# A decoder layer on one core: the prompt's threshold branch inside the sample's index stage, a projection between the first key tile's turn and its products, the gate's transposes one block later

## The chip, the cores and the metric

One core of a Trainium2 chip runs the whole kernel. The metric is device time in microseconds (us) for one execution; lower is better. The engines are named as in the profile: PE (TensorE), DVE (VectorE), ACT (ScalarE), POOL (GpSimd), SP (SyncE, which issues most transfers). PEld are PE's weight loads.

## The reference

One layer of a hybrid decoder for a prompt of 1024 tokens and for a sample step of 8 sequences with 4 new tokens each over a past of 8192 tokens. Model width 1024. The steps that matter here, cut from the reference:

```python
z = einsum('btd,de->bte', rmsnorm(x), w_in)       # qa ka va | qi ki wi | ga | qb kb vb gb
# group A: sparse attention
s = einsum('bqhd,bsd->bqhs', qi, ki) * 64**-0.5
score = einsum('bqh,bqhs->bqs', wi, relu(s)); score = where(valid, score, -inf)
idx = top_k(score, 256)                            # per query; the sample's keys come from paged cache_kidx
oa = softmax attention of qa over the gathered ka, va (with a bias by distance)
# group B: retention, 8 heads, chunks of 128, rotary angles on qb and kb
ob, state = chunked recurrence
y = concat(silu(ga) * oa, silu(gb) * head_norm(ob)) @ w_out
x = x + rmsnorm(y)
out = x + (p @ w_ple_up) * sigmoid(x @ w_ple_gate)
```

The outputs are y of prompt and sample, their k, v and index keys, and the retention states.

## The kernel before, in words

The layer is one program in five stages, here with their times in the profiled execution.

1. Norm, transposes, the index projections and the prompt's scores (0 to 172 us).
2. **The sample's index stage** (172 to 340). For each sequence `b` (8) and half `a` (2) an indirect gather on POOL brings 128 x 2048 past index keys into `kx` (two buffers). For each half tile `up` PE turns it (eight transposes into `ptx`, a pair of PSUM banks), ACT copies it to `kT`, PE multiplies it with the queries (two matmuls into `pox`) and ACT applies relu (`rl`). After four of these, `head_sum` weights and sums the heads (`py`), and `by_key` transposes the sums (`pxt`) and DVE copies them out (`xe`). `pox`, `pxt`, `pfl` and a few others share PSUM's tag "t", which has two banks, so a third user waits until the first has been read. Two other pieces of work are called in this loop at a set rate. `unit(rate)` advances a generator of projections (`proj_b`, PSUM tile `pb`, 24 matmuls each: qa, kava, ga). `step(bp)` advances `bisect_prompt`, which finds for each prompt query the threshold of its 256 best scores, on six query blocks at once, on DVE and for two of the six counts on ACT (`js`).
3. **Retention** (340 to 660): four pairs of heads, `hp` 0 to 3. Each has the projections of q and k (`pqk`, eight blocks, with the rotation `rp` on DVE and `qk` on POOL) and then of v and gate (`pvg`, eight blocks, each with its chunk: `ret`, `second`, `sm`, `sbd`). In `steps(hp)` run what is left of `bisect_prompt` (first pair) and the sample's own selection (`su`, `sjk`, `stot`, a branch at L965, comparisons L1194 and L1195, two running sums `cx` at L1203).
4. Attention (660 to 830), with gathers of the chosen keys on POOL.
5. Output projection (`po`) and gate (`pg`, `pu`), 830 to 1064. After the last column block of the output projection `finish_y(tb)` adds the residual and transposes the result with `split_T` for the gate's matmuls (`pty`).

`bisect_prompt` is a generator of 31 steps. Its last seven are: the flag `many` (PE reduces it into `pfl`, DVE reads it as `flp` and loads it into a register), then `tc.If(many > 0)` with 16 further counts, which the data does not call for, and `tb_`; and after it six mask blocks, one for each query block of 384 to 1024 keys. A block is a count and comparison (L727, L730), a running sum (L731, `rk`), three elementwise steps (L732, L733, L734) and small ones.

```python
            tickb[0] += 1.5          # L817: 16 passes, 24 steps of bisect_prompt in the index stage
            ...
        if hp == 0:
            step(bp, 2)              # L1420: the rest in retention's first pair
```

The order on each engine is not the order of the code. A scheduler places the instructions by its own estimate of times, within the dependences and the buffers; on the chip each engine then runs its queue strictly in that order and waits on semaphores. `tc.issue_after(ins)` adds an order without a wait: what is traced in its block comes behind `ins` on that engine.

Of the kernel before, what the change touches and what calls it, by code (L numbers as in the profile page):

```python
# [120 lines left out]
def tile_step(ctx: ExitStack, tc: tile.TileContext, I, O):  # L121
    nc = tc.nc
# [21 lines left out]
    def bank(name, tag="b"):  # L144
        if tag in kept.get("tags", ()):
            return kept["pool"].tile([128, 512], F32, tag="s", bufs=1, name=name)
        return psum["pool"].tile([128, 512], F32, tag=tag, bufs=psum["bufs"][tag], name=name)

    def pair(name):
        return psum["pool"].tile([128, 1024], F32, tag="S", bufs=psum["bufs"]["S"], name=name)  # L150
# [3 lines left out]
    def C(name, rows=128):  # L154
        o, w = _CW[name]
        return cst[:rows, o:o + w]

    ident = C("ident")
# [217 lines left out]
    tickb = [0.0]  # L376
# [83 lines left out]
    def unit(rate):  # L460
        tick[0] += rate
        while tick[0] >= 1:
            tick[0] -= 1
            next(unit_gen, None)
# [276 lines left out]
    def step(gen, n=1):  # L741
        for _ in range(n):
            next(gen, None)
# [45 lines left out]
    def later():  # L789
        if pend:  # L790
            pend.pop(0)()

    for b in range(8):
        rls = []
        for a in range(2):
            kx = sx.tile([128, 2048], F32, tag="kx", bufs=2, name="kx")
            nc.gpsimd.indirect_dma_start(
                out=kx, out_offset=None, in_=pages,
                in_offset=bass.IndirectOffsetOnAxis(ap=kidx[:, a * 8 + b:a * 8 + b + 1], axis=0))
            for up in range(2):  # L800
                pt = pair("ptx")
                kT = sx.tile([128, 1024], F32, tag="kT", bufs=2, name="kT")
                for u2 in range(2):
                    for i in range(4):
                        r2 = up * 8 + i * 2 + u2
                        c0 = u2 * 512 + i * 128
                        nc.tensor.transpose(pt[:, c0:c0 + 128], kx[:, r2 * 128:(r2 + 1) * 128], ident)
                nc.scalar.copy(kT, pt)
                po = bank("pox", "t")
                for u2 in range(2):  # L810
                    nc.tensor.matmul(po[u2 * 64:u2 * 64 + 64, :], qbd[:, b, :], kT[:, u2 * 512:u2 * 512 + 512],
                                     start=True, stop=True)
                rl = sx.tile([128, 512], F32, tag="rl", bufs=6, name="rl")
                nc.scalar.activation(rl, po, AF.Relu)
                rls.append(rl)
            later()
            tickb[0] += 1.5  # L817
            while tickb[0] >= 1:
                tickb[0] -= 1
                step(bp)  # L820
            unit(1.4)
        pend.append(lambda b=b, rls=rls: head_sum(b, rls))
    while pend:
        later()
# [597 lines left out]
    for hp in range(4):  # L1422
# [13 lines left out]
        for tb in range(8):  # L1436
            pt = bank("pqk")
# [9 lines left out]
        for tb in range(8):  # L1447
            pt = bank("pvg")
# [204 lines left out]
    pt = bank("ptys", "t")  # L1653
# [6 lines left out]
    x2 = [mr.tile([128, D], F32, tag="x2", bufs=9, name=f"x2_{tb}") for tb in range(9)]  # L1660
# [13 lines left out]
    def finish_y(tb):  # L1674
        rows = 128 if tb < 8 else NS
        src = (I["x_prompt"][0, tb * 128:(tb + 1) * 128, :] if tb < 8
               else I["x_sample"].rearrange("b t d -> (b t) d"))
        xt = mr.tile([128, D], F32, tag="xr", bufs=2, name="xr")
        nc.sync.dma_start(xt[:rows], src)
        y = x2[tb]  # L1680
        ss = mg.tile([128, 1], F32, tag="ss", bufs=2, name="ss2")
        nc.vector.tensor_reduce(ss[:rows], ssq[:rows, tb], axis=AX.X, op=ALU.add)
        r = rstd_of(ss, rows, 1.0 / D, f"y{tb}", mg)
        nc.vector.scalar_tensor_tensor(y[:rows], y[:rows], r[:rows], xt[:rows], op0=ALU.mult, op1=ALU.add)
        if tb < 8:
            x2T[tb] = split_T((y[:, :512], y[:, 512:]), 10 + tb)
        else:
            for a in range(2):
                pt = bank("ptxs", "t")
                for j in range(4):  # L1690
                    nc.tensor.transpose(pt[:, j * NS:(j + 1) * NS],
                                        y[:NS, a * 512 + j * 128:a * 512 + (j + 1) * 128], ident[:NS, :NS])
                nc.scalar.copy(x2sT[:, a * 4:a * 4 + 4], pt[:, :4 * NS].rearrange("p (j r) -> p j r", j=4))
# [23 lines left out]
    for cb in range(4):  # L1717
        cs = slice(cb * 256, (cb + 1) * 256)
        for tb in (8, *range(8)) if cb else (0, 1, 2, 3, 8, 4, 5, 6, 7):
            pt = bank("po2")  # L1720
            if tb < 8:
                mm_a(pt, tlhs(yT), wt[cb], 256, tb)
                take_y(tb, cb, pt[:, :256])
            else:
                sh = mm_s(pt, ysT, wt[cb], 256, mg, f"o{cb}")
                take_y(8, cb, sh[:, :256])
                wt.append(load_w(f"o{cb + 1}", [(w_out[:, (cb + 1) * 256:(cb + 2) * 256], 256)]) if cb < 3 else
                          load_w("g0", [(w_gate[:, 0:256], 256)]))
            if cb == 2:
                load_p(tb)  # L1730
            if cb == 3:
                finish_y(tb)

# [12 lines left out]
    for cb in range(4):  # L1748
        cur, curu = wg, wu
        cs = slice(cb * 256, (cb + 1) * 256)  # L1750
        for tb in (8, *range(8)):
            rows = 128 if tb < 8 else NS
            pg, pu = bank("pg"), bank("pu")
            sg = mg.tile([128, 256], F32, tag="sgm", bufs=2, name="sgm")
            if tb < 8:
                mm_a(pg, tlhs(x2T), cur, 256, tb)
                mm_a(pu, plhs, curu, 256, tb, kc=2)
                gsrc, usrc = pg[:, :256], pu[:, :256]
            else:
                gsrc = mm_s(pg, x2sT, cur, 256, mg, f"g{cb}")  # L1760
                nc.scalar.activation(sg[:rows], gsrc, AF.Sigmoid)
                usrc = mm_s(pu, psT, curu, 256, mg, f"u{cb}", kc=2)
                if cb < 3:
                    wg = load_w(f"g{cb + 1}", [(w_gate[:, (cb + 1) * 256:(cb + 2) * 256], 256)])
                    wu = load_up(cb + 1)
            if tb < 8:
                nc.scalar.activation(sg[:rows], gsrc, AF.Sigmoid)
            nc.vector.tensor_tensor(sg[:rows], usrc, sg[:rows], op=ALU.mult)  # L1768
            nc.vector.tensor_tensor(sg[:rows], sg[:rows], x2[tb][:rows, cs], op=ALU.add)
            dst = (O["y_prompt"][0, tb * 128:(tb + 1) * 128, cs] if tb < 8  # L1770
                   else O["y_sample"].rearrange("b t d -> (b t) d")[:, cs])
            nc.sync.dma_start(dst, sg[:rows])
# [38 lines left out]
```

## Time and profile before

| | us |
|---|---|
| median of three runs | 1076.75 |
| lowest, highest | 1073.38, 1078.46 |
| the profiled execution, time | 1065.73 |
| its span | 1063.9 |
| PE busy, share of the span | 991.7, 93% |
| DVE busy | 699.8, 66% |
| ACT busy | 504.2, 47% |
| POOL busy | 288.1, 27% |

The mean granted clock of PE is 0.973. A row of a group or an instruction gives the line, the engine, the operation, `out<-in` by the program's names (buffer numbers left out), the shapes, and in brackets the idle time of that engine just before it with what ended it. A row of waits gives the waiting instruction, what it waited for, the total in us, how often, and the longest. A row of stages gives the length of the stage, the busy us of PE, PEld, DVE, ACT and POOL with the number of instructions, then the granted clock of PE as a share of full speed.

### The profile page before, as it was taken

To read this page: it belongs to the slowest core of one execution; us is meant where nothing else is said; L and a number is where in the kernel's file an instruction comes from. 1 tells how busy PE (TensorE), PEld (TensorE's weight loads), DVE (VectorE), ACT (ScalarE), POOL (GpSimd) and SP (SyncE) were. 2 spreads that over 40 slices of the span, in tenths; PEclk is the share of its full clock that TensorE was granted. 3 is DMA by queue.
4 is the path that set the end of the run, shared out by engine and by line. 5 is a ranking of instruction groups with operands and counts; after the bars stand their busy time and mean duration, and the time that the engine had idled before them with its cause. 6 is when DMAs were issued, how large, how long until landed. Compare 5 with 4: busy or idle time off the path is not lost.

```text
span 1063.9 us, 19686 instructions
## 1 busy us (share of the span) xinstructions
PE 991.7 (93%) x7375; PEld 838.6 (79%) x7375; DVE 699.8 (66%) x2012; ACT 504.2 (47%) x1092; POOL 288.1 (27%) x287
## 2 busy tenths in 40 slices
PE   3899998998999789999989995999999999999998
PEld 2899997676776778898788893666656899989998
DVE  6847768999401798978986957887764424874332
ACT  5445554986434356842333435656544523442211
POOL 3102223111201532423632512634340521222100
PEclk8999999999999989999989996899999999999999
DMA  8211235546343311112201425623211312432211
GB/s 291 65 60 51 79 96 169 186 145 202 126 164 111 70 40 41 37 48 87 61 24 41 119 86 149 190 79 105 75 56 47 117 41 80 148 111 82 86 37 40
DMA packets 98308, 102.24 MB, mean 96 GB/s; under 512 B 21346, under 2 KB 88386, under 8 KB 95906
## 3 DMA queue, kind: packets, MB, share of 16 engines
q1 hardware_dynamic: 92450, 74.74, 23.3%
q0 software_dynamic: 5760, 26.22, 7.9%
q8 instruction: 58, 0.95, 0.4%
q14 instruction: 40, 0.33, 0.1%
HBM read 79.25 MB, written 21.68 MB: 95 GB/s over the span
## 4 chain that ended last, share of the span: by engine, by line
PE 53%; DVE 8%; ACT 2%; DMA 2%; issue 1%; POOL 1%; SPq 0%; DVEq 0%; ACTq 0%; POOLq 0%
PE ob L1587 4%; PE ptp L1579 4%; PE pg L265 3%; PE pg L267 3%; PE pg L266 3%; PE po L265 3%; PE po L266 2%; PE po L267 2%; PE pvg L265 2%; PE pvg L266 2%; PE pvg L267 2%; PE sa L1563 2%; PE sa L1564 2%; PE pqk L265 2%; PE pqk L266 1%; PE pqk L267 1%
## 5 line engine op out<-in xcount | busy, mean ns | idle before, releaser
L1147 POOL DMA_INDIRECT kvs<-in_cache_kv,idx x64 | 63.6, 994 | 84.1 <-ACT pT L1584 44.7
L265 PE MATMUL pqk<-whi_qkb,xh 128*128 128x256 f32 x256 | 74.5, 291 | 5.5 <-DVE rp L1036 5.5
L265 PE MATMUL pvg<-whi_vgb,xh 128*128 128x256 f32 x256 | 77.4, 302 | 1.6 <-DVE need L729 1.5
L266 PE MATMUL pvg<-wlo_vgb,xh 128*128 128x256 f32 x256 | 76.6, 299 | 0.0
L267 PE MATMUL pvg<-whi_vgb,xl 128*128 128x256 f32 x256 | 75.2, 294 | 0.0
L266 PE MATMUL pqk<-wlo_qkb,xh 128*128 128x256 f32 x256 | 73.5, 287 | 0.0
L265 PE MATMUL po<-whi_o,yTh 128*128 128x256 f32 x256 | 73.1, 286 | 0.4 <-DVE yaT L1598 0.4
L267 PE MATMUL pqk<-whi_qkb,xl 128*128 128x256 f32 x256 | 73.0, 285 | 0.0
L267 PE MATMUL po<-whi_o,yTl 128*128 128x256 f32 x256 | 72.8, 285 | 0.0
L265 PE MATMUL pg<-whi_g,yTh 128*128 128x256 f32 x256 | 72.7, 284 | 0.0
L266 PE MATMUL po<-wlo_o,yTh 128*128 128x256 f32 x256 | 72.7, 284 | 0.0
L267 PE MATMUL pg<-whi_g,yTl 128*128 128x256 f32 x256 | 72.3, 282 | 0.0
L266 PE MATMUL pg<-wlo_g,yTh 128*128 128x256 f32 x256 | 72.2, 282 | 0.0
L500 DVE SCALAR_TENSOR_TENSOR score<-r,wi,score 128x384 f32<-128x384 f32 (+5 forms) x42 | 44.2, 1053 | 21.0 <-ACT r L496 19.9
L1572 ACT ACTIVATE L<-L,mn 128x128 f32<-128x128 f32 (+7 forms) x64 | 49.5, 775 | 13.7 <-DVE mn L1569 13.6
L265 PEld LDWEIGHTS pqk<-whi_qkb,xh 128*128 128x128 f32 x256 | 48.2, 188 | 9.6 <-issue 6.8
L1768 DVE TENSOR_TENSOR sgm<-pu,sgm 128x256 f32<-128x256 f32 x32 | 13.5, 423 | 61.8 <-PE pu L267 58.6
L265 PEld LDWEIGHTS pvg<-whi_vgb,xh 128*128 128x128 f32 x256 | 50.6, 197 | 3.7 <-issue 1.7
L266 PEld LDWEIGHTS pvg<-wlo_vgb,xh 128*128 128x128 f32 x256 | 50.7, 198 | 0.5
L267 PEld LDWEIGHTS pvg<-whi_vgb,xl 128*128 128x128 f32 x256 | 50.6, 198 | 0.6
L265 PEld LDWEIGHTS po<-whi_o,yTh 128*128 128x128 f32 x256 | 49.0, 191 | 2.2 <-issue 1.6
L496 ACT ACTIVATE r<-si 128x384 f32<-128x384 f32 (+5 forms) x48 | 36.3, 758 | 30.3 <-PE si L354 29.0
(540 smaller groups left out, 3262.1 us busy)
## 6 DMA issues: line engine op xcount, KB each, us to landing
wraw_qkb<-in_w_in SPq DMA_DIRECT2D x16, 256.0 KB
wraw_vgb<-in_w_in SPq DMA_DIRECT2D x16, 256.0 KB
wraw_o<-in_w_out SPq DMA_DIRECT2D x8, 512.0 KB
qas<-qas_d SPq DMA_DIRECT2D x8, 512.0 KB
xr<-in_x_prompt SPq DMA_DIRECT2D x8, 512.0 KB
wraw_g<-in_w_ple_gate SPq DMA_DIRECT2D x8, 512.0 KB
out_y_prompt<-sgm SPq DMA_DIRECT2D x32, 128.0 KB
qas_d<-qst SPq DMA_DIRECT2D x8, 384.0 KB
```

The lines of the kernel that those rows point to most:

```text
L265: nc.tensor.matmul(pt[:, :n], ah, hi[:, k, :n], start=(k == 0), stop=False)
L266: nc.tensor.matmul(pt[:, :n], ah, lo[:, k, :n], start=False, stop=False)
L267: nc.tensor.matmul(pt[:, :n], al, hi[:, k, :n], start=False, stop=(k == kc - 1))
L496: nc.scalar.activation(r[:, :n], s[:, :n], AF.Relu)
L500: nc.vector.scalar_tensor_tensor(sc, r[:, :n], wi[:, qb, h:h + 1], sc, op0=ALU.mult, op1=ALU.add)
L1147: return nc.gpsimd.indirect_dma_start(out=dst, out_offset=None, in_=kvflat, in_offset=bass.IndirectOffsetOnAxis(ap=idx, axis=0))
L1563: nc.tensor.matmul(s[:, :wc], qas[:, h, :], kah[kv][:, c:c + wc], start=True, stop=False)
L1564: nc.tensor.matmul(s[:, :wc], qas[:, h, :], kal[kv][:, c:c + wc], start=False, stop=True)
L1572: behind[0] = nc.scalar.activation(L[:, :n], L[:, :n], AF.Exp, bias=least, scale=-1.0, accum_out=sm[:, i4:i4 + 1])
L1579: nc.tensor.transpose(tp[:, i4 * 128:i4 * 128 + 128], P[i4][:, kb * 128:kb * 128 + 128], ident)
L1587: nc.tensor.matmul(ob[64 * o:64 * o + 64, :256], vtok[:, kb, kv * 64:kv * 64 + 64], pT[:, o * 256:o * 256 + 256], start=(kb == 0), stop=(k ...
L1768: nc.vector.tensor_tensor(sg[:rows], usrc, sg[:rows], op=ALU.mult)
```

## The change

Three edits. In the first key tile (`b`, `a` and `up` all 0) one projection unit is called behind the eighth transpose, ahead of the products, and the call at the end of that pass is reduced by as much. The rate of `step(bp)` rises from 1.5 to 2.5, so that all 31 steps, with the branch and the six mask blocks, are issued within the 16 passes of the index stage. And `finish_y` is split: the transposes for the gate become `turn_y`, which is called one output block later.

```diff
                         c0 = u2 * 512 + i * 128
-                        nc.tensor.transpose(pt[:, c0:c0 + 128], kx[:, r2 * 128:(r2 + 1) * 128], ident)
+                        turned = nc.tensor.transpose(pt[:, c0:c0 + 128], kx[:, r2 * 128:(r2 + 1) * 128], ident)
                 nc.scalar.copy(kT, pt)
+                if b == 0 and a == 0 and up == 0:
+                    with tc.issue_after(turned.ins):
+                        unit(1.0)
                 po = bank("pox", "t")
...
-            tickb[0] += 1.5
+            tickb[0] += 2.5
             while tickb[0] >= 1:
                 tickb[0] -= 1
                 step(bp)
-            unit(1.4)
+            unit(1.4 if a or b else 0.4)
...
         nc.vector.scalar_tensor_tensor(y[:rows], y[:rows], r[:rows], xt[:rows], op0=ALU.mult, op1=ALU.add)
+
+    def turn_y(tb):
+        y = x2[tb]
         if tb < 8:
             x2T[tb] = split_T((y[:, :512], y[:, 512:]), 10 + tb)
...
             if cb == 3:
                 finish_y(tb)
+                if tb < 8:
+                    turn_y((8, *range(8))[tb])
...
+            if cb == 0 and tb == 1:
+                turn_y(7)
```

In the changed kernel the lines of the index stage from L811 on stand three lines lower. In the order of instructions the edits show at these places.

**The first key tile, PE.** Before, two whole projections (24 matmuls of the last 288 columns of qa, 24 of kava) stand ahead of the first transposes:

```order
L257 MATMUL pb<-xh,wlo_kava 128x384
L807 MATMUL ptx<-cst,kx 128x128 x16
L811 MATMUL pox<-kT,qbd 64x512 x2
L807 MATMUL ptx<-cst,kx 128x128 x8
L811 MATMUL pox<-kT,qbd 64x512 x2
L807 MATMUL ptx<-cst,kx 128x128 x8
```

Now, from the difference of the two, first the place where the eight transposes come in, ahead of the 288 columns of qa:

```order
 L256 MATMUL pb<-xl,whi_qa_1192 128x384
 L257 MATMUL pb<-xh,wlo_qa_1193 128x384
+L807 MATMUL ptx<-cst,kx 128x128 x8
 L255 MATMUL pb<-xh,whi_qa_1192 128x288
 L256 MATMUL pb<-xl,whi_qa_1192 128x288
```

and then the end of those columns, where the first products and sixteen transposes come in ahead of kava:

```order
 L256 MATMUL pb<-xl,whi_qa_1192 128x288
 L257 MATMUL pb<-xh,wlo_qa_1193 128x288
+L814 MATMUL pox<-kT,qbd 64x512 x2
+L807 MATMUL ptx<-cst,kx 128x128 x16
 L255 MATMUL pb<-xh,whi_kava 128x384
 L256 MATMUL pb<-xl,whi_kava 128x384
```

The 48 matmuls of the two projections have moved from ahead of the first transposes to behind them, qa's ahead of the first products and kava's behind the next sixteen transposes.

**The flag and the masks, DVE.** Before, all five remaining `xe` of the index stage, the first rotation of retention, and then the flag and the branch:

```order
L786 COPY xe<-pxt 128x4x4x4 x20
L882 MEMSET ssm 128x1
L924 MEMSET sgn 128x4
L925 MEMSET ssm 128x1
L846 COPY Xt<-newsc 32x32
L279 TENSOR_TENSOR sh_qk_3349<-pqk,sh_qk_3349 32x256 x3
L1034 TENSOR_TENSOR rp_0_3391<-pqk,cst 128x256
L1035 TENSOR_TENSOR rp_0_3392<-pqk,cst 128x4x32
L1036 TENSOR_TENSOR rp_0_3392<-pqk,cst 128x4x32
L626 TENSOR_SCALAR flp<-pfl 1x1
L627 TENSOR_LOAD flp
L709 COMPARE_AND_BRANCH
```

and behind the branch the masks alternate with the rotations and with the sample's selection (`sjk`, `su`):

```order
L732 SCALAR_TENSOR_TENSOR eq<-rk,need,eq 128x384
L1034 TENSOR_TENSOR rp_1_3719<-pqk,cst 128x256
L1035 TENSOR_TENSOR rp_1_3720<-pqk,cst 128x4x32
L1036 TENSOR_TENSOR rp_1_3720<-pqk,cst 128x4x32
L733 TENSOR_TENSOR gt<-gt,eq 128x384
L927 TENSOR_SCALAR sjk<-Xt 128x2080
L734 TENSOR_SCALAR mask<-gt 128x384
L730 TENSOR_SCALAR eq<-score,tbits 128x512
L1034 TENSOR_TENSOR rp_2_3796<-pqk,cst 128x256
L1035 TENSOR_TENSOR rp_2_3797<-pqk,cst 128x4x32
L1036 TENSOR_TENSOR rp_2_3797<-pqk,cst 128x4x32
L928 SCALAR_TENSOR_TENSOR su_3403<-sjk,Xt 128x2080
```

Now the flag follows the first of the five `xe`:

```order
L702 TENSOR_REDUCE cf<-ge 128x1
L706 TENSOR_REDUCE v<-pick 128x6
L786 COPY xe<-pxt 128x4x4x4 x4
L626 TENSOR_SCALAR flp<-pfl 1x1
L627 TENSOR_LOAD flp
L709 COMPARE_AND_BRANCH
```

and behind the branch come the blocks of 384, 512, 640 and 768 keys without a break, most of the block of 896, the second `xe`, and the rest:

```order
L730 TENSOR_SCALAR eq<-score,tbits 128x896
L727 TENSOR_SCALAR gt,cnt<-score,tbits 128x896
L731 SCALAR_TENSOR_TENSOR rk<-eq 128x896
L786 COPY xe<-pxt 128x4x4x4 x4
L729 TENSOR_SCALAR need<-cnt 128x1
L732 SCALAR_TENSOR_TENSOR eq<-rk,need,eq 128x896
L733 TENSOR_TENSOR gt<-gt,eq 128x896
L734 TENSOR_SCALAR mask<-gt 128x896
```

The last twelve copies of `xe` follow the block of 1024, and in retention's first pair DVE has the rotations and the sample's selection alone. On PE, the flag's matmul `pfl` stands among the sixteen transposes behind the `pxt` of that first `xe`. The `pox` that needs the bank of the next `pxt`, which stood directly behind another `pox`, now stands behind eleven more projection matmuls.

**The sample's selection, DVE.** The second running sum, before, in the values of pair 2:

```order
L1066 TENSOR_TENSOR sm<-ret,cst 128x128
L1066 TENSOR_TENSOR sm<-second,cst 128x128
L1218 TENSOR_TENSOR eq<-cx,eq 128x32x64
L1085 RECIPROCAL gy<-gy 32x2
L1463 COPY sbd_3314<-ret 64x64
L279 TENSOR_TENSOR sh_vg_6446<-pvg,sh_vg_6446 32x256
L1463 COPY sbd_3314<-ret 64x64
L1219 TENSOR_TENSOR sel<-sel,eq 128x32x64
L1086 TENSOR_TENSOR gz<-gy 32x2
L279 TENSOR_TENSOR sh_vg_6446<-pvg,sh_vg_6446 32x256
L1203 SCALAR_TENSOR_TENSOR cx<-sel 128x2112
```

and now, in the rotations of pair 2:

```order
L1222 TENSOR_TENSOR sel<-sel,eq 128x32x64
L1093 SCALAR_TENSOR_TENSOR gz<-bmv,gy 128x16
L1099 TENSOR_SCALAR acc_5376<-acc_5376,bmv,gy 128x64 x4
L1037 TENSOR_TENSOR rp_6_6387<-pqk,cst 128x256
L1038 TENSOR_TENSOR rp_6_6388<-pqk,cst 128x4x32
L1039 TENSOR_TENSOR rp_6_6388<-pqk,cst 128x4x32
L1206 SCALAR_TENSOR_TENSOR cx<-sel 128x2112
L1069 TENSOR_TENSOR sm<-ret,cst 128x128
```

It has moved ahead of the last rotations, and the two comparisons and the first running sum, which stood between the third and fourth rotation of pair 2, now stand at the seam from pair 1 to pair 2, among the last chunks' `sm` and `sbd` and the first rotation.

**Output projection and gate.** From about the fifth block of the output projection on, the rows and their waits are the same on every engine.

## The prediction

> **What bounds the kernel now.** I read the busy shares first, then the chain that ended last, then busy time by stage, then what TensorE (PE) waits for in each stage, and single rows last.
>
> ```profile
> PE 991.7 (93%) x7375; PEld 838.6 (79%) x7375; DVE 699.8 (66%) x2012; ACT 504.2 (47%) x1092; POOL 288.1 (27%) x287
> PE 53%; DVE 8%; ACT 2%; DMA 2%; issue 1%; POOL 1%; SPq 0%; DVEq 0%; ACTq 0%; POOLq 0%
> ```
>
> PE is busy 93% of the span and carries 53% of the chain; VectorE (DVE) comes next with 8%. None of the edits changes how much PE computes. So what can move is PE's idle time, about 72 us in all, and the time in which its clock is lowered after an idle stretch. The next view gives busy time by stage (columns PE, weight loads, DVE, ACT, POOL, then the granted clock).
>
> ```profile
> core 0: us, PE busy (x) PEld busy (x) DVE busy (x) ACT busy (x) POOL busy (x), PEclk, DMA share, GB/s
> 280.00:340.00 60.00, 59.03 (x372) 41.13 (x374) 2.61 (x18) 27.03 (x40) 10.44 (x16) 1.00 0.39 131
> 380.00:400.00 20.00, 17.25 (x112) 15.99 (x111) 19.79 (x48) 8.48 (x24) 5.52 (x6) 0.83 0.00 1
> 530.00:560.00 30.00, 25.57 (x172) 24.59 (x173) 23.37 (x53) 11.13 (x30) 10.76 (x8) 0.83 0.08 21
> ```
>
> The end of the index stage (280 to 340) has PE full and DVE almost empty: 57 us of free DVE. The first head pair of retention (380 to 400) has DVE full and PE idle, at a clock of 0.83. Moving DVE work from the second place to the first is therefore a sound exchange, if nothing in the first place starts to wait for DVE.
>
> **Term A, the first key tile.** PE's rows around it, then POOL's row for its gather and ACT's for the first copy:
>
> ```profile
> 171.47 0.30 PE L255 MATMUL pb<-xh,whi_qa 128*128 128x288 f32 x1
> 174.69 0.42 PE L255 MATMUL pb<-xh,whi_kava 128*128 128x384 f32 x1
> 178.62 0.34 PE L256 MATMUL pb<-xl,whi_kava 128*128 128x384 f32 x1
> 178.79 0.33 PE L257 MATMUL pb<-xh,wlo_kava 128*128 128x384 f32 x1
> 180.18 1.94 PE L807 MATMUL ptx<-cst,kx 128*128 128x128 f32 x16 [1.05 <-DMA kx<-in_cache_kidx,kidx]
> 186.90 1.98 PE L811 MATMUL pox<-kT,qbd 128*64 128x512 f32 x4 [4.78 <-ACT kT L808]
> ```
> ```profile
> 173.25 1.38 POOL L797 DMA_INDIRECT kx<-in_cache_kidx,kidx  x1 [0.57 <-issue]
> 185.84 1.01 ACT L808 COPY kT<-ptx 128x1024 f32<-128x1024 f32 x1
> ```
>
> From 171.47 to 179.13 PE runs 48 projection matmuls, 7.7 us, which cover the gather that is issued at 173.25 and lands at 180.18. In the new order the first eight transposes stand ahead of these 48. Nothing moves the gather, since the instructions ahead of it on POOL are the same. So PE stands idle from about 171.6 to 180.2: 8.6 us in place of 1.05, or 7.5 us more. In exchange the 24 matmuls of qa (171.47 to 174.7, 3.2 us) fill the 4.78 us in which PE waited for kT. kT itself can hardly come sooner, because in ACT's order it stays behind a count of the bisect, which waits for DVE; of DVE's work only a few short steps no longer stand ahead of it. The 24 of kava stand behind two more turns, where ACT's copies set the pace. Bounds: 0, if kava's 4.4 us also fall into ACT's pauses and the later waits of the stage take up the rest, and +9, which is all the 7.5 and 1.5 of lowered clock. The likeliest is 7.5 less 4.78, +3 us.
>
> **Term B, the six mask blocks in the index stage.** In the new order DVE takes the flag, the branch, the blocks for 384 to 896 keys up to the scan of 896, and only then the next xe. Rows of DVE, and the blocks by line:
>
> ```profile
> 276.64 0.20 DVE L706 TENSOR_REDUCE v<-pick 128x6 f32<-128x48 f32 x1
> 308.18 0.62 DVE L786 COPY xe<-pxt 128x64 f32<-128x64 f32 x4 [19.48 <-PE pxt L782]
> 344.54 0.14 DVE L626 TENSOR_SCALAR flp<-pfl 1x1 int32<-1x1 f32 x1
> 351.73 0.17 DVE L718 CAST gb<-v 128x6 int32<-128x6 f32 x1 [7.05 <-DVEq L709]
> ```
> ```profile
> L731 DVE TENSOR_TENSOR_SCAN rk<-eq 128x384 f32<-128x384 bf16 (+5 forms) x6 | 10.8, 1801 | 0.0
> L732 DVE SCALAR_TENSOR_TENSOR eq<-rk,need,eq 128x384 bf16<-128x384 f32 (+5 forms) x6 | 5.9, 988 | 0.0
> L727 DVE TENSOR_SCALAR_CACHE_REDUCE gt<-score,tbits 128x384 bf16<-128x384 f32 (+5 forms) x6 | 5.6, 936 | 0.0
> L730 DVE TENSOR_SCALAR eq<-score,tbits 128x384 bf16<-128x384 f32 (+5 forms) x6 | 3.7, 611 | 0.0
> L733 DVE TENSOR_TENSOR gt<-gt,eq 128x384 bf16<-128x384 bf16 (+5 forms) x6 | 3.6, 608 | 0.0
> L734 DVE TENSOR_SCALAR mask<-gt 128x384 bf16<-128x384 bf16 (+5 forms) x6 | 3.6, 601 | 0.0
> ```
>
> The six lines sum to 33.2 us. By width (384, 512, 640, 768 whole and some 0.6 of 896, which is 2842 of 4224 keys) about 22 us of it lie ahead of that xe. The branch costs DVE 7.2 us from flag to gb (344.54 to 351.73) with nothing computed. PE's rows where the flag and the next xe now stand:
>
> ```profile
> 288.94 1.91 PE L807 MATMUL ptx<-cst,kx 128*128 128x128 f32 x16
> 307.55 0.60 PE L782 MATMUL pxt<-cst,ys 128*128 128x128 f32 x4
> 311.55 1.94 PE L811 MATMUL pox<-kT,qbd 128*64 128x512 f32 x8
> ```
>
> pfl comes among the transposes at 288.94, so the flag is read at about 289.5 and xe comes at 289.5 + 7.2 + 22 = 319, in the clock of before. pxt lies in one of the two "t" banks, and the second product after it, which needs that bank, waits for xe. It is due at 311.55 + 1.0 (the first product) + 11 projection matmuls of 0.17 (178.62 to 178.79), or 314.4. So PE stalls about 4.5 us; 3 if the blocks run without pauses of other engines' making, 8 if they run as slowly as the widest ones here or a lowered clock follows, 0 if DVE gets there in time. I take +4. What is queued behind the waiting xe on DVE is only the rest of the masks and three more xe, whose pxt come later than the masks end.
>
> **Term C, retention's first head pair.** What PE waits for from 340 to 480 now, and the long DVE instruction that stays there:
>
> ```profile
> PE pqk L265 <- DVE rp L1036: 4.6, 3, 3.0
> PE stot L874 <- DVE sgn L912: 3.2, 2, 2.7
> PE pvg L265 <- DVE need L729: 1.5, 1, 1.5
> PE ret L1055 <- POOL qk L1039: 0.8, 1, 0.8
> ```
> ```profile
> 358.64 3.77 DVE L928 SCALAR_TENSOR_TENSOR su<-sjk,Xt 128x2080 uint16<-128x2080 uint16 x1
> ```
>
> These are 10.1 us. The 3.0 is the branch, the 1.5 a mask's own step, the 2.7 the sample's count behind a mask's scan: 7.2 us go for certain with the 40 us of DVE work (33.2 and the branch). The other 2.9 stand partly behind su, which stays; I take half, 1.4, and leave the rest. Then the clock: 0.83 over 20 us is 3.4 us lost, which goes with the waits that cause it. That makes -8.6 and -3.4, about -12, less 1 for what su will still hold back: -11 us. The bounds are -6 (certain waits, half of them replaced by a dependence behind them, and part of the clock) and -13.5 (all 10.1 and 3.4).
>
> **Term D, the sample's selection moves up by about half a head pair.** Both running sums of it (4.54 us each) and one PE stall:
>
> ```profile
> 503.67 2.29 DVE L1194 TENSOR_TENSOR eq<-X,tq 128x2048 bf16<-128x2048 f32 x1 [1.29 <-DMA X<-xs_d]
> 509.90 4.54 DVE L1203 TENSOR_TENSOR_SCAN cx<-eq 128x2112 f32<-128x2112 bf16 x1
> 540.60 4.54 DVE L1203 TENSOR_TENSOR_SCAN cx<-sel 128x2112 f32<-128x2112 bf16 x1
> 545.73 0.79 PE L1465 MATMUL ret<-sbd,qkT 128*128 128x128 f32 x2 [3.87 <-DVE sbd L1461]
> PE pqk L265 <- DVE rp L1036: 1.0, 1, 1.0
> ```
>
> The second scan, among the values (pvg) of pair 2, costs PE 3.87 us and up to 5.1 us of clock (0.83 over 30 us); the first, among the rotations (pqk), costs 1.0. In the new order the second stands among the rotations, where it should cost 1 to 1.5, and the first, with the two comparisons of 2.3 us ahead of it, at the seam from pair 1 to pair 2, where sbd still waits on DVE as it did at 545.73. So one stall goes (-4 to -9, I take -6) and one of the same kind may come (0 to +6, I take half): -3, bounds -9 and +3.
>
> **The rest.** The gate's transposes: from the fifth output block on, every engine's order and waits are the same in both kernels, so the split of finish_y is worth 0 whatever covers it. Attention holds the same instructions with PE full: 0.
>
> Sum: +3 + 4 - 11 - 3 = -7 us against the profiled execution, whose time is 1065.73 (span 1063.9). The three runs have their median at 1076.75, 11 us above it; the edits act on waits that the kernel has in each run, so I carry the difference over: **1069.8 us**, 0.65% less than before. About 0.5%, 5.4 us, is what a measurement of this kernel can tell from no change.
>
> **A rule that would change one term.** POOL's own rows show that it can be held up by DVE: its rotation product takes 0.46 us alone and 2.53 us beside su.
>
> ```profile
> 355.34 0.46 POOL L1038 TENSOR_TENSOR qk<-rp,rp 128x128 f32<-128x128 f32 x1 [0.46 <-DVE rp L1035]
> 360.20 2.53 POOL L1038 TENSOR_TENSOR qk<-rp,rp 128x128 f32<-128x128 f32 x1
> L797 POOL DMA_INDIRECT kx<-in_cache_kidx,kidx x16: 936/938/1383, 173.3 to 321.8; - x16
> ```
>
> The Trainium skill, "SBUF — State Buffer" (the box on DVE blocking DMA, and "Who interferes with whom"), says that both share a port under an exclusive lock, so that a gather issued by POOL cannot write its descriptors while certain DVE instructions run; by it the three gathers between 290 and 310 would now be issued late, beside the masks. Of the gathers the trace shows the contrary so far: 16 issues between 0.936 and 1.383 us, most of them beside a DVE busy with the bisect; beside these mask instructions none has run.
>
> **The rivals.**
> - *The wait moves instead of going (slower).* DVE's queue in the index stage: if the blocks keep the pace that they have now, interleaved with POOL's work, xe comes much later than 319. For the whole to end slower by 5.4 us the stall at 314.4 must be 4 + 7 + 5.4 = 16.4 us, so xe at 331 or later. The six lines whole, with the branch, give 289.5 + 7.2 + 33 = 330, the point from which it decides. For it: DVE is strictly in order and the scan is 10.8 us of the 33. Against: only two thirds stand ahead of xe. With A at its bound (+9) a stall of 10 is enough. Time: about 1083. Chance 0.20.
> - *Nothing is left.* A at +6, B at +6, D at 0, C at -11 give about 1078; the gain in retention is spent on PE in the index stage, which has no slack. Chance 0.20.
> - *More than forecast.* A and B at 0 (kava fills ACT's pauses, DVE is quicker), D at -6: 1076.75 - 17 = 1060. Chance 0.16.
> - *Gathers held up by the masks.* Three issues, each late by at most the longest mask step, a scan of about 2 us: +6 where all of it shows on PE, 1076. Against: kx has two buffers, so a gather is issued a tile ahead of its use. Chance 0.04.
> - *The forecast,* -3 to -11 us, 1066 to 1074: chance 0.40, three quarters of it beyond 5.4 us.
>
> Faster by over 0.5%: 0.30 + 0.16 = 0.46. Within: 0.10 + 0.20 + 0.04 = 0.34. Slower: 0.20. The range leaves out the ends of the first and third rival: 1060 to 1083; the likeliest case alone is 1066 to 1074.
>
> **What would show it.** A: PE's wait for kx at the first ptx about 8.6 us, the wait of pox for kT under 2. B: a wait of pox for xe of 3 to 6 us near 315 to 325, and a gap of 7 us behind the branch near 290. C: from 340 to 420 PE waits under 3 us and a clock near 1.00. D: no wait near 541 for sbd, and perhaps one near 495. The gate: the same waits as now (pty for DVE). The prediction is wrong if the stall for xe is over 10 us, if the waits in the first head pair stay although the masks have gone, or if new ones at the seam of pairs 1 and 2 exceed 6 us.

## The result: slower by 0.64%

| | before | after |
|---|---|---|
| median of ten runs, us | 1076.92 (1073.38 to 1079.69) | 1082.67 (1080.11 to 1084.92) |
| ratio, 95% interval | | 1.0064 [1.0045, 1.0082] |
| the profiled execution, time | 1065.73 | 1080.64 |
| its span | 1063.9 | 1078.8 |

The changed kernel is slower by 5.8 us, where 7 us less were forecast. The time lies at the upper end of the range that was given (1060 to 1083), and the sign is the other one. A second series of the same kernel (e12), timed with the last experiments, gave 1.0068 [1.0041, 1.0095]. One run of an experiment, 1563.3 us in e7 at a mean clock of 0.562, is slow and left out of its ratio.

One caution for everything below. The pair of profiled executions differs by 14.9 us, the medians by 5.8. The profiled execution of before lies 11 us under the median of its runs and is none of the ten; that of after is one of its ten, 2 us under their median. So a stage of the two profiles shows which wait came or went and about how much; the sum is settled by the runs.

The busy shares of the page of after, and its chain that ended last, answer to the first two rows of the prediction:

```profile
PE 993.7 (92%) x7375; PEld 842.5 (78%) x7375; DVE 702.6 (65%) x2012; ACT 501.3 (46%) x1088; POOL 290.2 (27%) x287
PE 42%; DVE 8%; DMA 2%; issue 2%; ACT 1%; POOL 1%; SPq 0%; ACTq 0%; DVEq 0%; POOLq 0%
```

PE does the same 7375 instructions in 2 us more of busy time. The other 13 us of span are idle time of PE. The next table says in which stage. It is worked out from PE's rows: a stage begins with the first `ptx`, the first `pqk`, the 289th matmul into `pqk` (it lies among the rotations of the second pair, pair 1, about 15 us behind their start), the first `sa` of attention, and the first `po`. Rows marked e are experiments, told further down; e1 is the kernel before and e12 the changed one, run again.

| us | index | retention into pair 1's rotations | rest of retention | attention | output and gate |
|---|---|---|---|---|---|
| before | 159.5 | 87.5 | 224.7 | 173.6 | 238.4 |
| before again (e1) | 159.7 | 87.7 | 222.8 | 173.7 | 239.1 |
| after | 166.0 | 79.8 | 231.8 | 181.3 | 239.7 |
| after again (e12) | 165.1 | 81.5 | 231.6 | 178.4 | 240.4 |
| projection alone (e2) | 165.8 | 86.8 | 223.6 | 177.2 | 242.5 |
| bisect's rate alone (e3) | 161.5 | 80.2 | 232.3 | 174.0 | 241.5 |
| gate alone (e4) | 160.1 | 88.7 | 223.6 | 173.8 | 238.9 |
| projection, two units ahead (e5) | 164.2 | 87.7 | 224.5 | 177.4 | 241.5 |
| projection, one unit ahead (e11) | 165.2 | 86.3 | 223.9 | 177.4 | 239.4 |
| after, two units ahead (e6) | 167.0 | 80.1 | 232.6 | 173.4 | 239.4 |
| rate, selection held (e7) | 160.7 | 79.4 | 222.7 | 176.7 | 242.6 |
| the same, two units ahead and projection (e8) | 165.2 | 79.7 | 224.7 | 177.1 | 243.1 |
| as e7, lower rate (e9) | 166.6 | 82.7 | 226.2 | 175.4 | 241.0 |
| as e7, order of the end kept (e10) | 162.1 | 79.9 | 227.7 | 173.6 | 239.3 |

Four columns move from before to after. The first part of retention gains 6 to 8 us, less than the 11 of term C. The index stage loses 5 to 7, the rest of retention 7 to 9, and attention 5 to 8.

### The profile page after: what moved, and what is told of

Same layout as the page of the kernel before. It is cut to its first block, busy times and chain, and to the rows that moved or that the text cites. A ratio compares the mean times of both kernels' runs of the same rounds, so it can differ in the third digit from the quotient of the medians.

```text
span 1078.8 us, 19699 instructions
## 1 busy us (share of the span) xinstructions
PE 993.7 (92%) x7375; PEld 842.5 (78%) x7375; DVE 702.6 (65%) x2012; ACT 501.3 (46%) x1088; POOL 290.2 (27%) x287
## 4 chain that ended last, share of the span: by engine, by line
PE 42%; DVE 8%; DMA 2%; issue 2%; ACT 1%; POOL 1%; SPq 0%; ACTq 0%; DVEq 0%; POOLq 0%
PE ob L1590 4%; PE ptp L1582 4%; PE pg L265 3%; PE pg L267 3%; PE pg L266 3%; PE po L265 3%; PE po L267 3%; PE po L266 3%; PE sa L1566 2%; PE sa L1567 2%; PE pvg L265 1%; PE pvg L266 1%; PE pvg L267 1%; PE pty L1637 1%; DVE oh L1249 1%
## 5 line engine op out<-in xcount | busy, mean ns | idle before, releaser
L1150 POOL DMA_INDIRECT kvs<-in_cache_kv,idx x64 | 67.7, 1058 | 73.8 <-ACT pT L1587 31.2
L267 PEld LDWEIGHTS pqk<-whi_qkb,xl 128*128 128x128 f32 x256 | 50.5, 197 | 2.5 <-issue 2.4
```

The costliest lines, as they stand in the source:

```text
L267: nc.tensor.matmul(pt[:, :n], al, hi[:, k, :n], start=False, stop=(k == kc - 1))
L1150: return nc.gpsimd.indirect_dma_start(out=dst, out_offset=None, in_=kvflat, in_offset=bass.IndirectOffsetOnAxis(ap=idx, axis=0))
```

## The experiments

All were timed in five rounds beside the kernel before on the same chip. The kernels named e1 to e4 split the change into its three edits; the kernel before itself was run among them as a control.

### One edit at a time

The control:

> The kernel before, unchanged, profiled a second time. The profiled execution of before (1065.73 us) lies 11 us under the median of its runs (1076.92), so a part of the 15 us between the two profiles may not belong to the change. Theory 1 (the change costs 6 us in the first key tile and some 9 at the sample's selection, and gains 8 in the first head pair): this profile shows the waits of the first one (kT 4.8, rp 4.6 and sgn 3.2 in the first pair, sbd 3.9 in pair 2) and is longer elsewhere. Theory 2 (the stall at the sample's selection is a matter of the execution): this profile shows a stall of 5 us or more between 455 and 480 us too, and PE waits in attention.

1071.62 against 1071.06 us, ratio 1.0009 [0.9988, 1.0029]. Theory 1 holds: the profile shows the waits of before again (4.98 us for `kT`, 3.9 for `sbd`) and none from 455 to 480 us.

The projection alone: the first hunk of the diff and `unit(1.4 if a or b else 0.4)`.

> The first edit alone: the projection behind the first eight transposes. Theory 1: PE waits 8.5 us for kx, the rest of the index stage runs 6 us later, nothing takes that back, so +5 to +6.5 us (ratio 1.005 to 1.006). Theory 2 (the later waits of the index stage take it up, and the difference comes from the selection): under +2 us.

1080.22 against 1071.06 us, ratio **1.0094 [1.0073, 1.0115]**: slower by 9.2 us, more than the whole change and more than theory 1 gave. Its index stage is 6.1 us longer than the control's, as theory 1 had it; attention and the last stage have about 3.5 us more each.

The rate of the bisect alone:

```diff
-            tickb[0] += 1.5
+            tickb[0] += 2.5
```

> The second edit alone: 2.5 steps a pass, so branch and masks in the index stage. Theory 1: no PE wait for xe, the first head pair gains 8 us, the sample's selection gives back 6 to 9, so -3 to +1 us. Theory 2: the gain stands, -6 to -9 us (ratio 0.992 to 0.994). Theory 3 (without the 6 us of the first tile xe comes too late and PE stalls on its bank): +2 or more, with a wait of pox for xe of 3 us.

1071.26 us, ratio 1.0007 [0.9988, 1.0027]: no change, although it moves 40 us of DVE work. This is theory 1, and its row in the table says why: -7 in one stage of retention, +8 to 9 in the next, +2 in the index stage.

The split of `finish_y` alone:

> The third edit alone: the gate's transposes one block later. All theories: the order of the last stage is the same, so within 1 us of before. If it is over 2 us slower, the seam between output projection and gate, where the profile of the changed kernel is 1 us longer, has a part in it.

1070.83 us, ratio 1.001 [0.9986, 1.0035]. It compiles to the order that the kernel before has, on every engine.

So the projection alone loses more than the whole change does, and the gain of the masks was given back one stage later. The two kernels with one edit add up to 9.4 us; the whole change has 5.8 and, in its second series, 8.0.

### What makes the projection dear

Two theories: PE stands idle for the gather of the first key tile, which the projections covered before; or the projection between the turn and the products delays what follows. To tell them apart, one or two units of projection are called ahead of the loop, so that the gather is covered again and the call between turn and products stays:

```diff
+    unit(2.0)                # e11: unit(1.0)
     ...                      # ahead of the loop over b
```

> The first edit alone, but two projection units are issued ahead of the loop, so that qa's last 24 matmuls and kava's first 24 stay ahead of the first transposes and it is a third unit (24 more of kava) that lies between turn and products. Attention's order is shuffled in the same places as by the first edit. Theory 1 (the loss is the gather that nothing covers): the wait for kx falls back to 1 us, the wait of pox for kT from 4.8 to under 1, and the kernel is 2 to 5 us faster than before (ratio 0.995 to 0.998). Theory 2 (two or more of the 9 us come from the shuffled attention stage, with its new wait of oS for PN): same as before or up to 3 slower, with the wait of 1.5 us for PN in the profile. Theory 3 (a projection between turn and products is itself harmful, because it delays the products and so ACT): slower by 4 or more.

1080.0 against 1070.8 us, ratio 1.0088 [1.0065, 1.011]: as slow as without the cover.

> The first edit with one unit issued ahead of the loop: qa's 24 matmuls stay ahead of the first transposes, kava's 24 lie between turn and products, and nothing is taken from later passes. Theory 1 (PE's idle time at the first tile is fixed by gather and copies, a projection only chooses which of the two waits it fills): wait for kx 5.4 us, wait for kT under 0.5, index stage 159 to 161 us as before; the kernel slower by attention's order alone, 1.003 to 1.006. Theory 3 (a projection between turn and products is harmful): index stage 163 us or more, 1.007 to 1.01.

1078.88 against 1071.09 us, ratio 1.0078 [1.0052, 1.0104]. In both the time is what theory 3 gave; the first theory, the uncovered gather, falls as the whole cause. PE's rows of e11, where its forecast of the two waits came true:

```profile
181.17 1.94 PE L808 MATMUL ptx<-cst,kx 128*128 128x128 f32 x8 [5.27 <-DMA kx<-in_cache_kidx,kidx]
194.64 1.08 PE L815 MATMUL pox<-kT,qbd 128*64 128x512 f32 x4
198.18 3.58 PE L815 MATMUL pox<-kT,qbd 128*64 128x512 f32 x8 [1.77 <-DVE kvs L410]
206.60 0.55 PE L408 MATMUL kvt<-cst,kvs 128*128 128x128 f32 x3 [1.78 <-ACT rl L818]
```

The wait for `kx` is 5.27 and the first product does not wait for `kT` at all, since the copy is done by 184.32; but the product starts at 194.64, behind two whole projections of 24 matmuls. In the control it starts at 189.04, after a wait of 4.98. And new waits follow, for `kvs` and `rl`. With two units ahead the wait for `kx` is about 1 us. The copy of `kT` is done by 188.64, and the first product starts at 203.20, behind projections and behind a `kvt` that waits for ACT:

```profile
202.37 0.90 PE L408 MATMUL kvt<-cst,kvs 128*128 128x128 f32 x3 [5.58 <-ACT kvs L404]
203.20 1.98 PE L815 MATMUL pox<-kT,qbd 128*64 128x512 f32 x4
```

The index stage is 165.8, 164.2 and 165.2 us with no, two and one unit ahead, against 159.7 in the control. What the three have in common is that the first product comes later than its `kT`, by 2.9, 14.6 and 10.3 us (in the control it follows at once), and which engine PE then waits for differs. That this place of the projection is the cause is argued from these rows: no kernel has the units ahead of the loop without the projection between turn and products, and the scheduler shifts other instructions too. The cover on the whole change:

> The changed kernel with the two units ahead of the loop, as above; everything else as changed. Theory 1: 8 to 11 us faster than the changed kernel, so 2 to 5 faster than before (0.995 to 0.998). Theory 2: about as before (1.000 to 1.003). If B is real when the index stage is not delayed, a wait of pox for xe of 1 to 3 us.

1075.47 against 1070.8 us, ratio 1.0026 [0.9999, 1.0053]. This is theory 2. By the ratios it is better than after (1.0064 and 1.0068, whose intervals overlap that of e6 a little), but not for the reason that was to be tested, and it shows no wait of `pox` for `xe`: its index stage has 167.0 us, and its attention 173.4 where after has 178 to 181. More on that below.

### What gives back the gain in retention

With the masks gone, the sample's selection runs earlier. To hold it back where it was, `steps` stops calling it for a while in the first pair and goes on in the second:

```diff
+    calls = [0]
     def steps(hp):
         with tc.high_priority():
-            step(bss if hp == 0 else ss)
+            if hp != 1 and (hp or calls[0] < 9):       # e10: < 10
+                step(bss if hp == 0 else ss)
+        if hp == 1 and calls[0] >= 17 + 11:
+            step(bss)
+        calls[0] += 1
...
-        if hp == 1:
+        if hp == 2:
```

> The second edit alone (branch and masks in the index stage), with the sample's selection held where it stood before: its last four steps are called in the values of pair 1 and the selection proper from pair 2 on, so the branch and both running sums have their old places among rotations and chunks. Theory 1 (the early selection gives back what the first pair gains): 5 to 8 us faster than before (0.9925 to 0.995), with the 8 us gained by 440 us kept to 640. Theory 2 (the loss behind 455 us comes with any place of the selection, because PE then works closer to DVE): as e3, within 2 us of before.

1067.26 against 1070.8 us, ratio **0.9972 [0.9956, 0.9988]**: the loss in the rest of retention is gone (222.7 us, with the rate alone 232.3), the gain before it stays (79.4). The whole gain is 3.5 us, less than the 5 to 8 of theory 1, as attention and the last stage have 3 to 4 us more each than the control. What PE waits for between 440 and 560 us, first in the kernel with the rate alone, then with the selection held:

```profile
PE ret L1465 <- DVE sbd L1461: 2.9, 1, 2.9
PE ret L1467 <- DVE sbd L1463: 2.4, 1, 2.4
PE second L1065 <- DVE sm L1066: 1.6, 2, 0.9
PE pvg L265 <- DVE rp L1036: 1.6, 1, 1.6
PE ret L1456 <- DVE sbits L983: 0.4, 1, 0.4
```
```profile
PE pqk L265 <- DVE bst L1075: 2.0, 1, 2.0
PE ret L1473 <- DVE sbd L1469: 1.8, 1, 1.8
```

8.9 us of waits become 3.8.

> The held selection and the covered first tile together, without the third edit. Theory 1: the sum of the two, 7 to 12 us faster than before (0.989 to 0.9935). Theory 2: within 3 us of before.

1072.97 us, ratio 1.0016 [1.0, 1.0031]: with the projection (two units ahead) the held selection is 5.7 us slower than without it, mostly in the index stage (165.2 against 160.7). This is theory 2.

### The rate, the masks' place and the order of attention

Two more settings of the hold: a rate of 2.2 in place of 2.5, and one more step called before the pause, with which the order from attention to the end is row for row that of before.

> As e7 (selection held), with 2.2 steps a pass in place of 2.5. The selection stands where it stands in e7; the masks come one xe later; and the scheduler lays attention out in the order of e6, whose profile had attention 3 us shorter than e7's (173.4 against 176.7 us from first sa to first po). Theory 1 (an edit upstream changes the order in attention, and that order alone costs 3 us and more): attention 173 to 174 us, 0.993 to 0.996 of before. Theory 2 (attention's length varies by the execution, not by the order): 176 to 178 us again in about half of such cases, and 0.997 as e7.

1072.5 against 1071.09 us, ratio 1.0013 [0.9993, 1.0033]. A rate lower by 0.3 puts the flag behind the second `xe`, and now the wait that term B forecast is there, in DVE's and PE's rows:

```profile
340.00 0.61 DVE L786 COPY xe<-pxt 128x64 f32<-128x64 f32 x4
340.76 1.66 PE L811 MATMUL pox<-kT,qbd 128*64 128x512 f32 x6 [3.29 <-DVE xe L786]
```

The index stage has 166.6 us, 5.9 more than e7, and the gain is lost. Attention's 175.4 us lie between the two theories: PE has its instructions in e6's order, but waits 2.0 us for a gather there, where e6 waits 0.95.

> As e7 with 2.5 steps a pass and one more step of the selection in the first pair: the branch of the selection stands three chunks' sm earlier, its running sums one rotation earlier, and the order from the first sa to the end is that of the kernel before, row for row. Theory 1: attention 173.7 us as before, the first pair 8 us shorter, so 0.992 to 0.996, the fastest of all. If the seat of the selection's branch matters by itself (among the chunks of pair 1), the stretch behind 440 us gives back 2 to 4 us and the ratio is 0.996 to 0.999.

1065.23 against 1071.09 us, ratio **0.9954 [0.9935, 0.9973]**: faster than both kernels. It has the bisect's rate, no projection between turn and products, the selection held, and attention at 173.6 us. The second clause of its expectation holds in part: with the branch at another seat the rest of retention has 227.7 us, 5 more than e7.

> The changed kernel again, on the chip of these runs, for a second profile of it. Theory 1: index stage 166 us, first pair 80, the stretch behind it 232, as in the first profile; attention 177 us (the 181.3 of the first profile has 4 us that belong to that execution). Ratio 1.005 to 1.008.

1079.08 against 1071.09 us, ratio 1.0068 [1.0041, 1.0095]. Its stages came out as expected, within 1.5 us each.

## Why the prediction was wrong, term by term

Two steps failed most: term D followed two running sums where the whole selection moved, and attention was put at 0 though its order had changed. In A and C the sign was right and the size was off; B came to nothing, by its entry for the branch.

**A, the first key tile: forecast +3, measured +5.4 to +6.5.** The step for the gather came true to a tenth: 8.6 us were forecast, with `kT`'s 4.78 filled by qa. PE's rows of after:

```profile
180.20 1.94 PE L807 MATMUL ptx<-cst,kx 128*128 128x128 f32 x8 [8.54 <-DMA kx<-in_cache_kidx,kidx]
185.79 1.08 PE L814 MATMUL pox<-kT,qbd 128*64 128x512 f32 x4
193.88 1.08 PE L814 MATMUL pox<-kT,qbd 128*64 128x512 f32 x4 [0.90 <-ACT kT L808]
197.71 1.06 PE L807 MATMUL ptx<-cst,kx 128*128 128x128 f32 x8 [0.72 <-DMA kx<-in_cache_kidx,kidx]
203.20 1.08 PE L814 MATMUL pox<-kT,qbd 128*64 128x512 f32 x4 [1.30 <-DVE kvs L410]
```

The reading of `kT` was wrong: "kT itself can hardly come sooner", but its copy came 3.6 us sooner (185.84 before):

```profile
182.23 1.01 ACT L808 COPY kT<-ptx 128x1024 f32<-128x1024 f32 x1
```

So the first product, at 185.79 behind qa, came 2.5 us later than its data. And the step behind the first tile was mis-sized: the likeliest value, 7.5 less 4.78, put nothing for lowered clock and for new waits in the rest of the stage. Stage rows, first of before and then of after: the 30 us ahead of the first `ptx`, and 60 us in the middle of the index stage (PE's busy time is the second number, its clock the last but two):

```profile
150.00:180.20 30.20, 29.14 (x169) 27.55 (x168) 23.20 (x32) 14.60 (x21) 7.19 (x6) 1.00 0.36 115
220.00:280.00 60.00, 56.48 (x347) 41.98 (x348) 52.54 (x131) 40.61 (x64) 9.74 (x7) 1.00 0.48 156
```
```profile
150.00:180.20 30.20, 21.66 (x121) 20.13 (x120) 23.12 (x37) 12.26 (x18) 2.90 (x4) 0.94 0.36 115
220.00:280.00 60.00, 55.55 (x334) 40.63 (x332) 53.35 (x133) 38.37 (x62) 10.23 (x7) 0.97 0.50 164
```

7.5 us of PE's work (29.14 - 21.66) have gone from ahead of the first turn into the index stage. There the wait of 4.78 goes; about 1.8 us are lost to the clock in the middle (0.03 of 60); and the waits of the stage other than `kT`'s first one grow by about 2 us, since its idle time falls only from 11.8 to 9.0. 7.5 - 4.78 + 1.8 + 2.0 = 6.5, the difference of the stage. The prediction had the first two numbers; the other 3.8 us are what it left out. The experiments e5 and e11 show that the 7.5 is not to be had back by covering the gather from the front: other waits then take its place, at the same length of the stage.

**B, the masks in the index stage: forecast +4, measured no wait of `pox` for `xe`.** DVE's rows of after:

```profile
295.53 0.14 DVE L626 TENSOR_SCALAR flp<-pfl 1x1 int32<-1x1 f32 x1 [0.88 <-PE pfl L624]
297.05 0.17 DVE L718 CAST gb<-v 128x6 int32<-128x6 f32 x1 [1.37 <-DVEq L709]
315.92 2.02 DVE L731 TENSOR_TENSOR_SCAN rk<-eq 128x896 f32<-128x896 bf16 x1
317.86 0.59 DVE L786 COPY xe<-pxt 128x64 f32<-128x64 f32 x4
```

The blocks take 20.8 us (297.05 to 317.86; 22 forecast). The branch takes 1.37 us, where the row of before had 7.05, and this was the step that failed: DVE is 5.7 us earlier for it. The second product, which needs the bank, stands at 320.92, 2.5 us behind the end of `xe`; in e3, without the projection, the slack is 2.5 us too. With a branch of 7.05 in this place the same rows would give a wait of about 3 us (318.45 + 5.7 - 320.92), an estimate near the forecast. The mechanism itself is real, as e9 shows with its wait of 3.29. The rate alone costs the index stage 1 to 2 us (e3, e7). So B was mis-sized by its entry for the branch, which had been taken over from another place in the program as if it were a property of the instruction.

**C, retention's first pair: forecast -11, measured -6 to -8.** The stage row of after:

```profile
380.00:400.00 20.00, 18.46 (x154) 17.48 (x153) 13.60 (x42) 15.26 (x35) 6.47 (x9) 1.00 0.19 51
```

The clock is 1.00 where it was 0.83, and DVE has 13.60 us of work in place of 19.79. (After stands 6.5 us later here, so the two rows are not quite the same work.) What PE still waits for between 344 and 440:

```profile
PE pqk L265 <- DVE rp L1039: 3.5, 2, 2.0
PE stot L877 <- DVE sgn L915: 1.5, 1, 1.5
PE ret L1459 <- DVE sm L1069: 1.5, 1, 1.5
```

6.5 us are left of about 10, more than the under 3 that the prediction named as its mark, so "7.2 us go for certain" was the step that failed: the rotations and the sample's count still queue behind the selection's own long instructions. Over the column PE's idle time falls by 3.0 us only (9.6 to 6.6); the other 4.7 are shorter busy time, at a mean clock of 0.98 in place of 0.96.

**D, the sample's selection: forecast -3, measured +7 to +9.** This is the largest miss of a term that was priced. The prediction followed the two running sums and nothing else. But the whole selection moves, and with it its branch and its last two counts, now among pair 1's chunks. DVE's rows of after:

```profile
468.49 0.22 DVE L984 SCALAR_TENSOR_TENSOR ssm<-ssm 128x1 f32<-128x1 f32 x1 [3.27 <-DVEq L968]
469.56 2.35 DVE L864 TENSOR_SCALAR_CACHE_REDUCE sjk<-Xt,sbits 128x2080 bf16<-128x2080 f32 x1
474.76 2.34 DVE L992 TENSOR_SCALAR_CACHE_REDUCE sjk<-Xt,sbits 128x2048 bf16<-128x2048 f32 x1
498.11 4.53 DVE L1206 TENSOR_TENSOR_SCAN cx<-eq 128x2112 f32<-128x2112 bf16 x1
```

In before the same wait behind the branch was 0.9 us. PE's waits in after between 455 and 520 follow. The first row stands at the seam with the first running sum (505.63), the other two among the chunks, next to the branch (468.96 and 459.67):

```profile
PE ret L1468 <- DVE sbd L1464: 2.9, 1, 2.9
PE ret L1459 <- DVE sbits L986: 2.0, 1, 2.0
PE second L1068 <- DVE sm L1069: 1.1, 1, 1.1
```

and in the 20 us around the branch, before and then after:

```profile
455.00:475.00 20.00, 20.00 (x163) 18.83 (x162) 14.17 (x46) 10.44 (x33) 5.18 (x3) 1.00 0.09 25
```
```profile
455.00:475.00 20.00, 16.89 (x116) 15.21 (x116) 14.24 (x50) 6.02 (x20) 3.68 (x4) 0.91 0.02 5
```

Over the whole column PE's idle time grows from 12.1 to 17.0 us and its busy time by 2.2, with the clock at 0.95 in place of 0.96. The single wait of 3.87 for `sbd` that was to go did go; its place is taken by those above, 2.3 more for `sbd` further on, and smaller ones. That the selection's place is the cause is shown by e7: with the masks where after has them and the selection held, the column is back at 222.7 us (e3, which differs by the hold alone, 232.3). The other three held kernels have 224.7 to 227.7, the four that are not held 231.6 to 232.6.

**Attention: forecast 0, measured +5 to +8.** "Attention holds the same instructions with PE full: 0" was the error, a term put at nothing without a reason from the order. The instructions are the same, but in every kernel in which the first or second edit moved work upstream, e10 alone excepted, the scheduler set them in another order. PE's rows at the end of attention in e2:

```profile
830.17 0.40 PE L1355 MATMUL ppt<-cst,pr 64*128 64x64 f32 x3
832.10 0.40 PE L1370 MATMUL oS<-vnew,PN 32*64 32x128 f32 x2 [1.49 <-DVE PN L1367]
```

and the same step in before, where the products `ob` of the other attention still stand between `ppt` and `oS`:

```profile
819.15 0.40 PE L1352 MATMUL ppt<-cst,pr 64*128 64x64 f32 x3
819.54 0.65 PE L1587 MATMUL ob<-pT,vtok 128*64 128x256 f32 x4
820.12 0.66 PE L1579 MATMUL ptp<-cst,L 128*128 128x128 f32 x4
820.71 0.65 PE L1587 MATMUL ob<-pT,vtok 128*64 128x256 f32 x4
821.77 0.43 PE L1367 MATMUL oS<-vnew,PN 32*64 32x128 f32 x2
```

In before that chain of short steps has cover; in e2 and in after it stands last and uncovered. After waits besides, for its gathers and their copies, between 658 and 839:

```profile
PE pkg L1327 <- issue: 1.5, 1, 1.5
PE oS L1370 <- DVE PN L1367: 1.5, 1, 1.5
PE pkw L1332 <- ACT kgT L1328: 1.1, 1, 1.1
PE pkg L1327 <- DMA kvs<-in_cache_kv,idx: 1.0, 1, 1.0
```

None of the four stands among the waits of before. Kernels with the order of before have 173.6 to 173.8 us here (before, e1, e4, e10), five with orders of e2's kind 176.7 to 177.4. All eight kernels of that kind show the wait for `PN`, 1.48 or 1.49 us, and none of the other six does. But e3 is of that kind too, with PE's order that of e11, and has 174.0: its first wait in the stage, for `mn`, is 5.27 us where the other seven have 7.89. And another order need not be slower: e6 has a third one and 173.4 (e9, with the same on PE, 175.4). No kernel changed the order of attention alone, so its price of 3.5 us is read from the rows and not isolated; e10 differs from e7 in other stages too. After's further 1 to 4 us are the waits for gathers and copies, which differ between its two profiles.

**The gate: forecast 0, measured 0** (e4). After and e3, with and without the third edit, have the same order on every engine from the first `po` on. The last column varies from 238.4 to 243.1 us without a cause that the runs show.

**The rivals.** The time is that of "the wait moves instead of going", but its mechanism, a wait for `xe` past 331 us, did not happen: DVE was done with the second `xe` at 318.5. That the rival's time was met is luck. Gathers held up by the masks did not show either. PE's only waits for `kx` in after are the 8.54 and the 0.72 above, both before any mask runs, and POOL's issues from 285 to 315, three of them beside the masks, have a median of 954 ns and at most 1112, where the sixteen of before had 936 and 1383:

```profile
L797 POOL DMA_INDIRECT kx<-in_cache_kidx,kidx x4: 938/954/1112, 285.1 to 314.2; - x4
```

By the port lock of the Trainium skill, "SBUF — State Buffer" ("Who interferes with whom"), such an issue could be held up by DVE; the four here show no such delay.

In sum, for the profiled pair: +6.5 in the index stage (A, with B at nearly nothing), -7.7 (C), +7.1 (D), +7.7 in attention and +1.3 at the end make the 14.9 us of its span. The medians have 5.8 to 8.0 of that. Why the profiled execution of before lies so far under the median of its ten runs was not found; beside the experiments, runs of the same kernel went from 1065.46 to 1074.98, and 1065.73 is within that.

## What to carry to other kernels

When work is taken off a busy stage, list everything that moves up into the space, branch and counts and not only the longest instructions, and price what stands in *its* new place: a gain of 7 to 8 us was given back one head pair later, and a hold of a few lines kept it there. Where a scheduler sets the order, stages that no line of the diff touches can be re-ordered as well; compare the order to the end before one writes 0. And work that fills a wait is not free if it stood in front of a chain: moved behind the first turn, it stood here in front of products whose data were ready, and the stage stayed as long with the first wait covered as without.

## What the hardware showed that was not expected

The time that DVE loses behind a branch that is not taken depends on where the branch stands. For the first branch it is 6.2 to 7.3 us among retention's rotations (before, e1, e2, e4, e5, e11) and 1.36 to 1.4 at the end of the index stage (all kernels with the higher rate). For the second it is 0.8 to 0.9 at its old place and when held, and 3.2 to 3.3 in the four kernels where the selection runs early. The waits for DVE's queue in before and in after:

```profile
DVE gb L718 <- DVEq L709: 7.1, 1, 7.1
DVE ssm L981 <- DVEq L965: 0.9, 1, 0.9
```
```profile
DVE gb L718 <- DVEq L709: 1.4, 1, 1.4
DVE ssm L984 <- DVEq L968: 3.3, 1, 3.3
```

Both branches skip the same instructions in both kernels. The traces have more on this than the waits. They hold the times of the DMA transfers, among them, in before, 40 packets of 8192 bytes on a queue that the profile calls "q14 instruction". In each of the ten long waits behind a branch, over all kernels, one such packet falls inside the wait (before: wait from 344.68 to 351.73, packet at 349.40; after: 465.22 to 468.49, packet at 466.48). In none of the eighteen short ones does one; there the next packet comes after the wait has ended (after: wait to 297.05, packet at 297.83). So the long waits go with a load of instructions, and where the branch stands would decide whether the instructions behind it are there already. No kernel was run to test this, and the traces do not say for which engine a packet is.
